# A hybrid mLSTM and convolution step on one core: other weight sums, places and pairings for the modulation and gate units of the first feed-forward

## The chip, the cores and the metric

The kernel runs on one core of a Trainium2 chip. Its engines are TensorE (PE; PEld is its weight load), VectorE (DVE), ScalarE (ACT), GpSimd (POOL) and SyncE (SP), which issues DMAs. Each works through its own queue in order; DMAs are issued from SP's and from POOL's queue. The metric is the device time of one execution in microseconds, the median of the runs.

## The reference, cut to what matters

One layer works on 128 context tokens and 512 latent tokens, 640 in all, of width 1024. The context is modulated with `c_ctx`, the latent tokens with `c`.

```python
mod = silu(cond) @ w_mod + b_mod                # 1024 x 9216, in nine chunks of 1024
sh1, sc1, g1, shm, scm, gm, sh2, sc2, g2 = split(mod, 9)
h = modulate(rmsnorm(x, norm_g[0]), sh1, sc1)
x = x + 0.5 * g1 * swiglu(h, ffn1_w1, ffn1_w2)  # D_FF = 2816
h = modulate(rmsnorm(x, norm_g[1]), shm, scm)
y = mixer(h, ...)                               # mLSTM and short convolution, merged, @ w_o
x = x + gm * y
h = modulate(rmsnorm(x, norm_g[2]), sh2, sc2)
x = x + 0.5 * g2 * swiglu(h, ffn2_w1, ffn2_w2)
y = rmsnorm(x, final_norm)

def modulate(h, shift, scale): return h * (1 + scale) + shift
def swiglu(h, w1, w2): a, b = split(h @ w1, 2); return (silu(a) * b) @ w2
```

So `shm` and `scm` are due when the first feed-forward ends, `g1` when its second matrix is multiplied, and `sh2` only after the mixer.

## The kernel before, in words

**Products.** Everything is kept with the features on the partitions and the 640 tokens along the free axis, in two halves of 320. Each float32 operand is split into a high and a low part (`split`, L75 the cast on ScalarE, L79 the difference on VectorE), and three matmuls of 320 columns (`three`, L288 to L290) make one float32 product.

**Pairs.** Most of the weights are multiplied two column blocks of 128 at a time (`pair_el`), by a two-by-two block scheme with seven products in place of eight (`pair_steps`): A11, S1, S2, A12, S3, S4, A22, each 4 x 3 = 12 matmuls, 84 a pair. S1 = A21 + A22, S2 = S1 + A11, S3 = A11 + A21 and S4 = A12 + S2 are sums of weight blocks, made by VectorE (L270; in the convolution's pairs S1 and S3 by GpSimd). The right side of each is a block of the activations, whose tile tells in the trace which product runs: H11, T1, T2, H21, T3, H22, T4. The products gather in four PSUM banks. S3 and A22 add into the same bank, and between the two the bank is read: by VectorE (L360), or, where the pair has `spare_v`, by ScalarE into a tile that VectorE then adds to. In the pairs of the second matrix the read is VectorE's L325, in `gated_sum`, unless `spare_v` is set.

**Summed pairs.** A pair marked `summed` gets S1 and S3 from the DMA: `pair_loads` loads two 256 KB quarters into a tile from SP's queue, adds two more to them with accumulating DMAs from POOL's queue (both L235), loads the first block (L218) as ever and the last quarter into a tile of its own, `wq`.

**Loads.** Weights come into a ring of five buffers of 512 KB (`wr`), in the order of the program; a load is issued when the buffer five places before it was given up (`load_more`). Splits are queued four products ahead of their use (`cast_more`, AHEAD = 4), so that in S3's step of a pair VectorE's queue gets the next pair's splits and sums ahead of L360.

**Modulation units.** A chunk of `mod` is computed half by half, in units of one 512 KB load of `w_mod` (L620). There are two ways. On VectorE (`mod_dve`): a unit has four steps, each a multiply-add over 512 columns into an accumulator (L765, L767); after a half's fourth unit TensorE adds up the partitions (L776), turns the result (L784), and VectorE adds the bias (L792). On TensorE (`mod_half`, wide, used by `with_own` for `g1`): a unit has two matmuls with 32 columns each (L649), in strips of 32 rows of one bank; even units use the first two strips, odd units the last two. In both ways the unit's load is put behind the loads of the pair that carries it and takes a place in the ring until its last step.

**Where steps go.** An element's `fill` is a list of steps; a pair issues them spread over its seven products, so that after product i some `len * i / 7` of them have been queued. `with_units` puts units into elements by the numbers in `places` and their closing steps (sum, turn, bias) into the elements after them.

**The first feed-forward** (`ffn`, called at the line that makes `head, els`) takes the 22 column blocks of the hidden layer in groups of 8, 8 and 6. In the first group three of the hidden blocks belong to the head, and five pairs follow; the first four carry the eight `g1` units. Each group of eight is multiplied with the second matrix in four pairs (`w2s`), whose results are added to `x` in DRAM by accumulating DMAs from POOL's queue (`x_add`, L1029). The last group has six pairs, 351.8 to 444.6 us in the trace, of which the third to the sixth are summed. In the first of them the last two `x_add` go out, and in the third `x` is loaded back (`x_in`, L2081, eight loads of 320 KB). Then five plain blocks of the second matrix and one element of three blocks in halves follow. Five halves made on VectorE, two of `shm`, two of `scm` and the first of `sh2`, are spread over all this as `places` says.

**The convolution** stands behind the mLSTM, 940 to 1113 us in the trace: ten pairs for its inputs (`bg_pair`, `cx_pair`) and four for a gate (`gsc_pair`).

Of the kernel before, what the change touches and what calls it, by code (L numbers as in the profile page):

```python
# [14 lines left out]
KT = 8  # L15
# [29 lines left out]
def mixer_step(ctx: ExitStack, tc: tile.TileContext, x_prompt, x_sample, state_C, state_n, state_m,  # L45
# [109 lines left out]
    def raw(n):  # L155
        load_more()
        return rtile[n]
# [40 lines left out]
    def step(fn):  # L198
        return element([], [], fn)
# [175 lines left out]
    def pair_el(load1, load2, ev, e1=None, spare_v=False, acts=HB, at=None, calm=False, gated=None,  # L375
                summed=False):
        po = pair_ops(summed, e1)
        at = at or {}

        def emit():  # L380
            nf = len(fill)
            for i, _ in enumerate(pair_steps(ORDER, ev, spare_v, acts, gated)):
                if not calm:
                    relax(7 - i if i else 9)
                drain(nf - nf * (i + 1) // 7)
                for f in at.get(i, ()):
                    f()
        return dict(element(pair_loads(load1, load2, summed), [po[name] for name in ORDER], emit), pair=True)
# [320 lines left out]
    def with_own(pairs, ch, *last):  # L709

        us, fs = zip(*[mod_half(ch, half, True) for half in range(2)])
        out = []
        for p, el in enumerate(pairs):
            el = dict(el, raws=list(el["raws"]))
            fill = []
            for i in (2 * p, 2 * p + 1) if p < 4 else ():
                load, unit_ = us[i // 4][i % 4]
                at_ = len(el["raws"])
                el["raws"].append(load)

                def go(unit_=unit_, at_=at_, el=el):
                    unit_(raw(el["base"] + at_))
                    rdone.add(el["base"] + at_)
                    load_more()
                fill += [step(go), step(lambda: None)]
            if p == 2:
                fill[1] = step(fs[0][0])
                fill[3:] = [step(f) for f in fs[0][1:]]
            if p == 4:
                fill = [step(fs[1][0]), step(lambda: None)] + [step(f) for f in (*fs[1][1:], *last)]  # L730
            el["fill"] = fill
            out.append(el)
        return out
# [68 lines left out]
    def with_units(main, units, spare=0, places=None):  # L802

        out = []
        n, m = len(main) - spare, len(units)
        e = 0
        post = []
        due = [sum(places[:i + 1]) for i in range(len(main))] if places else None
        for i, el in enumerate(main):
            el = dict(el, raws=list(el["raws"]), fill=list(el.get("fill", ())))  # L810
            now, post = post[:1], post[1:]
            if places:
                el["fill"], now = el["fill"] + now, []
            while e < m and (e < due[i] if places else e * n < (i + 1) * m):
                load, fns, more = units[e]
                at_ = len(el["raws"])
                el["raws"].append(load)
                for j, fn in enumerate(fns):
                    def go(fn=fn, at_=at_, el=el, last=(j == len(fns) - 1)):
                        fn(raw(el["base"] + at_))  # L820
                        if last:
                            rdone.add(el["base"] + at_)
                            load_more()
                    el["fill"].append(step(go))
                post += [step(f) for f in more]
                e += 1
            el["fill"] += now
            out.append(el)
        assert e == m
        return out + [step(lambda: lazy.extend(p["emit"] for p in post))]  # L830
# [212 lines left out]
    def eights(w1, w2, g, f0, n_head, head, more, back, sums, w2sums, pops_):  # L1043
# [76 lines left out]
        for m in range(0, KT, 2):  # L1120
            rows_ = lambda i, m=m: (tile_of((m + i) % 4), modT[:, g, m + i, 0:1])

            def ev(mi, h, src, m=m):
                y = tile_of((m + mi) % 4)
                if h and m == KT - 2:
                    PO["x_end"].append(lambda: x_add(m + mi, y))
                    return
                if h:
                    x_add(m + mi, y)
                    return  # L1130
                for a, b, cd in ((0, P, 1), (P, HT, 0)):
                    A.activation(y[:, a:b], src[:, a:b], AF.Copy, scale=modT[:, g, m + mi, cd:cd + 1])
            at = {}
            if m == 0:
                four = lambda k: lambda: put_lent("T4", k, raw2(k))
                at = {0: [lambda: relax_some(2)], 1: [relax], 2: [lambda: put_lent("T3", 3, raw3(3)), four(0)],
                      3: [four(1), four(2)], 4: [four(3)]}
            elif m == KT - 2 and back:
                at = {4: [lambda: h_back("T3")], 6: [lambda: h_back("T4")]}
            w2s.append(pair_el(w_load(w2, f0 * P, 8, m * P, D), w_load(w2, f0 * P, 8, (m + 1) * P, D), ev,  # L1140
                               acts=UB, at=at, gated=rows_, spare_v=m == 0, summed=m in w2sums))
        return grp, w2s

    def ffn(w1, w2, g, lists, head_of, n_head, groups, more, sums, w2sums, pops):
# [338 lines left out]
    def more_of(p):  # L1483
        return {0: {p: {0: [lambda: h_away("T3", "T4")]}}, 1: {0: {4: [x_end]}},
                2: {0: {4: [x_end, lambda: PO.pop("xs")]}, 2: {1: [x_whole]}}}
    head, els = ffn(ffn1_w1, ffn1_w2, G1, after_lists(1, SHM), first_head, 3, (8, 8, 6), more_of(4),
                    ({4, 5, 6, 7}, {4, 5, 6, 7}, {2, 3, 4, 5}), {0, 2}, {0: (2, 2, 1), 1: (2, 2, 1), 2: (3, 2)})
    PO["ma_x"] = ExitStack()

    def gate_weights_():  # L1490
# [5 lines left out]
    def ma_wide():  # L1496
# [3 lines left out]
    els[0][1][0] = dict(els[0][1][0], first=[open_ma, gate_weights_])  # L1500
    w2s = els[2][1]
    prog += with_units(els[0][1] + els[1][0] + els[1][1] + els[2][0] + w2s[:-1],
                       mod_dve(SHM, (0, 1), ma_wide) + mod_dve(SCM, (0, 1), ma_wide) + mod_dve(SH2, (0,), ma_wide),
                       places=[0, 2, 1, 0] + [1, 0, 0, 0, 1, 0, 0, 0] + [0, 2, 1, 1] + [1] * 6 + [1] * 5)
    prog += [step(gain(1, SCM)), step(lambda: PO["ma_x"].close()), w2s[-1]]


# [418 lines left out]
    def cx_pair(m):  # L1926
        def ev(mi, h, src):
            if mi == 0:
                CV["c", h] = t = t3()
                A.activation(t, src, AF.Identity, bias=bias(C_OFF + m * P))  # L1930
                return
            u = CV["c", h]
            V.scalar_tensor_tensor(u, src, bias(X_OFF + m * P), u, op0=OP.add, op1=OP.mult)
            if h == 0:
                CV[m] = xp.tile([P, T], F32, name="x", bufs=KT)
            uc = CV[m][:, hsl(h)]
            w0, w2 = col("cw", m), col("cw", 2 * KT + m)

            def mid():
                A.activation(uc, u, AF.Identity, scale=col("cw", KT + m), bias=col("cb", m))  # L1940

            def side(o, i, lo, hi, w):
                def f():
                    a, b = (o[:, :, 1:], i[:, :, :-1]) if lo else (o[:, :, :-1], i[:, :, 1:])
                    V.scalar_tensor_tensor(a, b, w, a, op0=OP.mult, op1=OP.add)
                return f
            segs = [(uc, u)] if h else [(uc[:, P:], u[:, P:])]
            segs = [(a.rearrange("p (r w) -> p r w", w=GW), b.rearrange("p (r w) -> p r w", w=GW))
                    for a, b in segs]
            if h == 0:  # L1950
                segs.append((uc[:, None, :P], u[:, None, :P]))
            lazy.insert(h, mid)
            for o, i in segs:
                lazy.extend([side(o, i, True, False, w0), side(o, i, False, True, w2)])
        return z_load(C_OFF + m * P), z_load(X_OFF + m * P), ev
# [77 lines left out]
    def bg_pair(m):  # L2033
        def ev(mi, h, src):
            uc = CV[m + mi][:, hsl(h)]
            V.scalar_tensor_tensor(uc, src, bias(B_OFF + (m + mi) * P), uc, op0=OP.add, op1=OP.mult)

            def put_b():
                PB[m + mi, h] = bpair()
                split(uc, *PB[m + mi, h])  # L2040
            lazy.append(put_b)
        return z_load(B_OFF + m * P), z_load(B_OFF + (m + 1) * P), ev
# [63 lines left out]
    ml[0]["fill"] = [step(f) for f in r_ins[6:]] + ml[0]["fill"] + [step(lambda: None)] * 5  # L2106
    prog.append(step(g_load(0)))
    prog += with_units(ml, mod_dve(GM, (1,), m_wide) + mod_dve(SH2, (1,), m_wide))
    for m in range(0, KT, 2):
        if m:  # L2110
            prog += [pair_el(*cx_pair(m), G), pair_el(*cx_pair(m + 1), G)]
        prog.append(pair_el(*bg_pair(m), G, spare_v=True))
    prog += weave([pair_el(*gsc_pair(m)) for m in range(0, KT, 2)], [step(lambda: None)] * 3 + [step(t_in(0))])
    y_acts = lambda k, h: YB[k, h]
    sc = [plain_el(w_load(w_sc_out, 0, KT, m * P, D), KT, lambda k, h: PB[k, h], sc_ev(m)) for m in range(KT)]
    for m in range(KT - 1):
# [126 lines left out]
```

## Time and profile before

| | |
|---|---|
| runs | 1665.88, 1674.21, 1669.24 us; median 1669.24 |
| profiled execution | 1670.03 us, its span 1667.9 us |
| mean granted TensorE clock | 0.993 |
| PE, DVE, ACT, POOL busy | 1628.7, 1301.8, 881.7, 337.7 us |
| bytes moved | 251.83 MB, 151 GB/s in the mean |

An instruction's row has its start, its length, engine, line, operation, and the tiles as out<-in; numbers of buffers are left out, so that `ps` is any product bank, `ax` any small one, `wr` any buffer of the ring, `ws` a sum of weights, `wh` and `wl` the halves of a split. A bracket behind it is the idle time of the engine before it and what ended that. Groups of waits name the waiting line, the line waited for, the total in us, the number of waits and the longest. The end of a matmul is modelled, and successive matmuls overlap, so starts are compared with starts.

### The profile page before, as it was taken

What the parts mean: (1) busy time and instruction counts of PE and PEld (TensorE: products, weight loads), DVE (VectorE), ACT (ScalarE), POOL (GpSimd) and SP (SyncE); (2) the same over time, 40 slices, a digit from 0 to 9 for tenths busy, and PEclk for the clock granted to TensorE, in tenths of its full rate; (3) what the DMA queues carried; (4) which work ended last, traced back from release to release, by engine and by line L of the source; (5) the groups of instructions that cost most, each with busy time, mean ns of one, the idle gap of its engine ahead of it and who ended that gap; (6) DMA issues with size and microseconds to landing.
All of it is one profiled execution on the core that took longest, in us unless ns stands there. A gap on an engine that the chain in (4) does not pass through costs nothing.

```text
span 1667.9 us, 29682 instructions
## 1 busy us (share of the span) xinstructions
PE 1628.7 (98%) x10997; PEld 1577.0 (95%) x10997; DVE 1301.8 (78%) x2730; ACT 881.7 (53%) x1953; POOL 337.7 (20%) x465
## 2 busy tenths in 40 slices
PE   8999999997989999999999999999999999999998
PEld 5989999997988999999999999999999999999998
DVE  6868878876768778787887788869778876786765
ACT  5656555643437665454653355642366665565443
POOL 2132311132011241111212222001123113113102
PEclk9999999998999999999999999999999999999999
DMA  9698966798535352343338532347558768468621
GB/s 322 182 239 171 222 151 130 174 215 215 154 94 177 95 134 69 92 107 83 105 92 298 148 89 77 104 137 227 153 161 182 144 147 199 96 150 184 180 80 63
DMA packets 339600, 251.83 MB, mean 151 GB/s; under 512 B 12019, under 2 KB 312442, under 8 KB 339456
## 3 DMA queue, kind: packets, MB, share of 16 engines
q1 hardware_dynamic: 280432, 169.89, 35.6%
q0 software_dynamic: 58992, 80.05, 22.5%
q8 instruction: 86, 1.41, 0.3%
q14 instruction: 58, 0.48, 0.1%
q10 hardware_dynamic: 32, 0.01, 0.0%
HBM read 213.62 MB, written 36.28 MB: 150 GB/s over the span
## 4 chain that ended last, share of the span: by engine, by line
PE 82%; DVE 8%; DMA 4%; ACT 4%; issue 2%; POOL 0%; SPq 0%; ACTq 0%; DVEq 0%; POOLq 0%
PE ps L288 25%; PE ps L289 24%; PE ps L290 24%; DMA wr<-in_ffn_w_dram 4%; DVE wl L79 2%; PE ax L1789 2%; PE ax L1820 2%; DVE ma L767 1%; PE ax L1792 1%; ACT wh L75 1%; DVE ws L270 1%; PE ax L1766 1%; ACT Uh L930 0%; DVE x L1016 0%; DVE HT4l L79 0%
## 5 line engine op out<-in xcount | busy, mean ns | idle before, releaser
L79 DVE TENSOR_TENSOR wl<-wr,wh 128x512 fp32r<-128x512 f32 (+1 forms) x401 | 277.7, 702 | 104.2 <-ACT wh L75 101.3
L75 ACT CAST wh<-wr 128x512 fp32r<-128x512 f32 (+1 forms) x403 | 238.3, 606 | 53.5 <-DMA wr<-in_ffn_w_dram 28.5
L79 DVE TENSOR_TENSOR wl<-ws,wh 128x512 fp32r<-128x512 f32 x300 | 207.0, 690 | 64.3 <-ACT wh L75 63.4
L75 ACT CAST wh<-ws 128x512 fp32r<-128x512 f32 x300 | 184.4, 621 | 94.2 <-DVE ws L270 82.1
L288 PE MATMUL ps<-HT4h,wh 128*128 128x320 f32 x440 | 140.7, 320 | 15.9 <-DVE t L360 13.2
L235 POOL DMA_DIRECT2D wr<-in_ffn_w_dram x56 | 72.7, 1469 | 329.8 <-DMA wr<-in_ffn_w_dram 167.2
L289 PE MATMUL ps<-HT4l,wh 128*128 128x320 f32 x440 | 137.7, 313 | 0.6 <-DVE HT4l L79 0.5
L288 PE MATMUL ps<-Uh,wh 128*128 128x320 f32 x440 | 138.2, 314 | 0.0
L290 PE MATMUL ps<-HT4h,wl 128*128 128x320 f32 x440 | 137.2, 312 | 0.0
L289 PE MATMUL ps<-Ul,wh 128*128 128x320 f32 x440 | 136.7, 311 | 0.0
L290 PE MATMUL ps<-Uh,wl 128*128 128x320 f32 x440 | 136.3, 310 | 0.0
L288 PE MATMUL ps<-HT3h,wh 128*128 128x320 f32 x388 | 121.8, 314 | 0.2
L288 PE MATMUL ps<-H11h,wh 128*128 128x320 f32 x376 | 119.1, 317 | 0.8 <-ACT H11h L75 0.8
L289 PE MATMUL ps<-HT3l,wh 128*128 128x320 f32 x388 | 119.9, 309 | 0.0
L290 PE MATMUL ps<-HT3h,wl 128*128 128x320 f32 x388 | 119.9, 309 | 0.0
L289 PE MATMUL ps<-H11l,wh 128*128 128x320 f32 x376 | 116.8, 311 | 0.7 <-DVE H11l L79 0.4
L288 PE MATMUL ps<-H21h,wh 128*128 128x320 f32 x376 | 117.5, 312 | 0.0
L290 PE MATMUL ps<-H11h,wl 128*128 128x320 f32 x376 | 116.3, 309 | 0.0
L290 PE MATMUL ps<-H21h,wl 128*128 128x320 f32 x376 | 116.2, 309 | 0.0
L289 PE MATMUL ps<-H21l,wh 128*128 128x320 f32 x376 | 115.9, 308 | 0.0
L288 PE MATMUL ps<-H22h,wh 128*128 128x320 f32 x344 | 107.7, 313 | 0.0
L289 PE MATMUL ps<-H22l,wh 128*128 128x320 f32 x344 | 106.4, 309 | 0.4
(489 smaller groups left out, 4954.2 us busy)
## 6 DMA issues: line engine op xcount, KB each, us to landing
wr<-in_ffn_w_dram SPq DMA_DIRECT2D x90, 512.0 KB, 5.8
wr<-in_w_in_dram SPq DMA_DIRECT2D x72, 512.0 KB, 3.9
wr<-in_w_mod_dram SPq DMA_DIRECT2D x59, 512.0 KB, 5.0
xd<-x POOLq DMA_DIRECT2D x56, 320.0 KB, 7.2
wr<-in_ffn_w_dram SPq DMA_DIRECT2D x60, 256.0 KB, 4.6
wr<-in_ffn_w_dram POOLq DMA_DIRECT2D x56, 256.0 KB, 5.3
x<-xd POOLq DMA_DIRECT2D x24, 320.0 KB, 7.7
wq<-in_ffn_w_dram SPq DMA_DIRECT2D x28, 256.0 KB, 3.2
```

The source lines that it names most:

```text
L75: A.copy(hi, raw)
L79: V.tensor_sub(lo, raw, f32(hi))
L235: queue.dma_start(t[:, 512 * o:512 * o + 512].rearrange("p (k n) -> p k n", k=4), dap(w, (row0 + 512 * half) * ncol + col0, [[ncol, P], [P ...
L270: engine.tensor_add(t, part(o, a), part(o, b))
L288: PE.matmul(ps, hi[:, ws], ah, start=start, stop=False, skip_group_check=True)
L289: PE.matmul(ps, hi[:, ws], al, start=False, stop=False, skip_group_check=True)
L290: PE.matmul(ps, lo[:, ws], ah, start=False, stop=stop, skip_group_check=True)
L767: V.scalar_tensor_tensor(acc, w_, s, acc, op0=OP.mult, op1=OP.add)
L1766: PE.matmul(p[:, :P], S["k", dt][:, sl], S["q", dt][:, sl], start=(dt == 0), stop=(dt == 1))
L1789: PE.matmul(p2[:, :DH + 1], S["q", dt][:, sl], S["C"][d][:, dt, :], start=(dt == 0), stop=(dt == 1))
L1792: PE.matmul(p1[:, :DH + 1], S["p", ch][:, d, :], PO["vt"][:, ch, :], start=True, stop=True)
L1820: PE.matmul(p[:, :DH + 1], kw[:, dt * P:(dt + 1) * P], PO["vt"][:, ch, :], start=True, stop=True)
```

## The change

It touches two places of the program. In the first feed-forward:

- Gate units in twos (`with_own`): the two `g1` units of a pair are issued in one step, behind the fifth product (in the third pair the fourth), not behind the second and the sixth. The steps that close the first half are moved with them.
- Modulation units early (`with_units`): where `places` is given, three empty steps follow each unit's four, so that a single unit's steps are queued behind the first four products of a pair, not behind the second, fourth, sixth and seventh.
- No DMA sums in the last group: its pairs load two blocks each, and VectorE makes all four sums.
- `spare_v` is set in two more of the four pairs of the second matrix in the groups of eight (`m` = 2 and 4).
- The four units of `sh2`'s first half leave the first feed-forward, and `places` is thinned: none in the last pair of the second group's second matrix, none in the last group's sixth pair, and the five plain blocks have one in the first three only.

In the convolution, these four units are put into the four `bg_pair` elements, with accumulators from the pool of `x` tiles; their closing steps go into the gate's pairs.

```diff
@@ with_own @@
             fill = []
-            for i in (2 * p, 2 * p + 1) if p < 4 else ():
-                load, unit_ = us[i // 4][i % 4]
+            if p < 4:
+                units = us[p // 2][2 * (p % 2):2 * (p % 2) + 2]
                 at_ = len(el["raws"])
-                el["raws"].append(load)
-
-                def go(unit_=unit_, at_=at_, el=el):
-                    unit_(raw(el["base"] + at_))
-                    rdone.add(el["base"] + at_)
+                el["raws"] += [load for load, _ in units]
+
+                def go(units=units, at_=at_, el=el):
+                    tiles = [raw(el["base"] + at_ + i) for i in range(2)]
+                    for i in range(2):
+                        units[i][1](tiles[i])
+                    rdone.update((el["base"] + at_, el["base"] + at_ + 1))
                     load_more()
-                fill += [step(go), step(lambda: None)]
+                fill = [step(lambda: None), step(go), step(lambda: None)]
             if p == 2:
-                fill[1] = step(fs[0][0])
-                fill[3:] = [step(f) for f in fs[0][1:]]
+                fill[0] = step(fs[0][0])
+                fill[2:] = [step(f) for f in fs[0][1:]]
@@ with_units @@
                 post += [step(f) for f in more]
+                if places:
+                    el["fill"] += [step(lambda: None)] * 3
                 e += 1
@@ eights @@
-                               acts=UB, at=at, gated=rows_, spare_v=m == 0, summed=m in w2sums))
+                               acts=UB, at=at, gated=rows_, spare_v=m == 0 or m < KT - 2 and 2 in w2sums, summed=m in w2sums))
@@ first feed-forward @@
-                    ({4, 5, 6, 7}, {4, 5, 6, 7}, {2, 3, 4, 5}), {0, 2}, {0: (2, 2, 1), 1: (2, 2, 1), 2: (3, 2)})
+                    ({4, 5, 6, 7}, {4, 5, 6, 7}, ()), {0, 2}, {0: (2, 2, 1), 1: (2, 2, 1), 2: (3, 2)})
@@
-                       mod_dve(SHM, (0, 1), ma_wide) + mod_dve(SCM, (0, 1), ma_wide) + mod_dve(SH2, (0,), ma_wide),
-                       places=[0, 2, 1, 0] + [1, 0, 0, 0, 1, 0, 0, 0] + [0, 2, 1, 1] + [1] * 6 + [1] * 5)
+                       mod_dve(SHM, (0, 1), ma_wide) + mod_dve(SCM, (0, 1), ma_wide),
+                       places=[0, 2, 1, 0] + [1, 0, 0, 0, 1, 0, 0, 0] + [0, 2, 1, 0] + [1, 1, 1, 1, 1, 0] + [1, 1, 1, 0, 0])
@@ convolution @@
+    conv = []
     for m in range(0, KT, 2):
         if m:
-            prog += [pair_el(*cx_pair(m), G), pair_el(*cx_pair(m + 1), G)]
-        prog.append(pair_el(*bg_pair(m), G, spare_v=True))
-    prog += weave([pair_el(*gsc_pair(m)) for m in range(0, KT, 2)], [step(lambda: None)] * 3 + [step(t_in(0))])
+            conv += [pair_el(*cx_pair(m), G), pair_el(*cx_pair(m + 1), G)]
+        conv.append(pair_el(*bg_pair(m), G, spare_v=True))
+    conv += weave([pair_el(*gsc_pair(m)) for m in range(0, KT, 2)], [step(lambda: None)] * 3 + [step(t_in(0))])
+    prog += with_units(conv, mod_dve(SH2, (0,), m_wide), places=[1, 0, 0] * 3 + [1] + [0] * 4)
```

## The prediction

> **What bounds the kernel now.** First the page: is one engine full, and where is it not?
>
> ```profile
> span 1667.9 us, 29682 instructions
> PE 1628.7 (98%) x10997; PEld 1577.0 (95%) x10997; DVE 1301.8 (78%) x2730; ACT 881.7 (53%) x1953; POOL 337.7 (20%) x465
> PEclk9999999998999999999999999999999999999999
> ```
>
> PE works for all but some 39 us, so work taken off the other engines pays only where PE waits for them. The granted clock dips in one slice, the tenth (375 to 417 us), inside the first feed-forward's last group. Next the waits, of PE alone, to see who makes it wait:
>
> ```profile
> PE ps L288 <- DVE t L360: 13.2, 4, 6.1
> PE ax L776 <- DVE ma L767: 4.5, 3, 3.2
> PE ps L288 <- DVE x L325: 2.1, 4, 0.8
> ```
>
> Three VectorE lines hold PE for 19.8 us, and the change touches all three. Then the table by stretches, with bounds put where PE's timeline shows matmuls of one pair or one gap. Columns: length, then busy time (and count) of PE, PEld, DVE, ACT, POOL; granted clock, DMA share, GB/s.
>
> ```profile
> 351.80:444.55 92.75, 79.52 (x519) 77.86 (x517) 61.91 (x114) 39.39 (x85) 20.80 (x26) 0.94 0.78 194
> 376.25:384.85 8.60, 3.84 (x15) 3.84 (x16) 5.30 (x10) 4.28 (x9) 3.26 (x6) 0.80 0.74 186
> 395.12:405.51 10.39, 4.29 (x18) 4.29 (x18) 6.42 (x12) 4.30 (x9) 2.64 (x2) 0.67 0.77 178
> 404.60:418.00 13.40, 13.40 (x94) 12.80 (x93) 9.46 (x18) 5.71 (x13) 0.00 (x0) 0.97 0.68 164
> 418.00:432.20 14.20, 12.78 (x88) 12.51 (x87) 10.19 (x19) 5.79 (x13) 2.57 (x2) 1.00 0.72 158
> 473.16:483.84 10.68, 5.82 (x24) 4.46 (x25) 7.02 (x15) 2.31 (x6) 2.53 (x4) 0.68 0.51 143
> 965.70:978.00 12.30, 12.30 (x86) 12.30 (x85) 10.82 (x20) 7.81 (x17) 2.87 (x2) 1.00 0.32 87
> 978.00:990.30 12.30, 12.30 (x86) 12.30 (x85) 11.95 (x21) 6.87 (x15) 2.83 (x2) 1.00 0.30 85
> 990.30:1002.60 12.30, 12.30 (x86) 12.30 (x85) 10.08 (x18) 6.58 (x14) 3.15 (x2) 1.00 0.33 87
> ```
>
> An undisturbed pair (965.70) is 12.30 us for 84 matmuls (two more overlap its edges): 0.146 us a matmul, 1.76 us a product of twelve. The last group's six pairs should take 6 x 12.30 = 73.8 us; they take 92.75. The two worst stretches follow in PE's, VectorE's and SyncE's timelines and in the chain:
>
> ```profile
> 381.01 0.42 PE L288 MATMUL ps<-HT4h,wh 128*128 128x320 f32 x1 [4.76 <-DVE t L360]
> 401.22 0.64 PE L288 MATMUL ps<-HT4h,wh 128*128 128x320 f32 x1 [6.10 <-DVE t L360]
> ...
> 378.66 0.69 DVE L79 TENSOR_TENSOR wl<-wr,wh 128x512 fp32r<-128x512 f32 x1 [6.85 <-ACT wh L75]
> 380.48 0.48 DVE L360 TENSOR_TENSOR t<-ps,t 128x320 f32<-128x320 f32 x1
> 385.58 0.74 DVE L767 SCALAR_TENSOR_TENSOR ma<-wr,cm,ma 128x512 f32<-128x512 f32 x1
> 398.21 0.69 DVE L79 TENSOR_TENSOR wl<-wr,wh 128x512 fp32r<-128x512 f32 x1 [8.01 <-ACT wh L75]
> ...
> 386.35 0.37 SPq L218 DMA_DIRECT2D wr<-in_ffn_w_dram  x1
> ...
> 386.35 11.18 DMA wr<-in_ffn_w_dram
> ```
>
> Read backwards: PE needs the bank that L360 reads; L360 stands in VectorE's queue behind the next pair's split, which waits for ScalarE's cast, which waits for a load. That load is issued at 386.35, the moment the modulation unit's last step (385.58 to 386.32) gives its buffer up, and takes 11.18 us to land. So the bound here is the ring of five buffers: a step queued behind a pair's seventh product keeps a load out.
>
> **The change part by part.** The profiled execution took 1670.0 us (span 1667.9 and 2.1 around it), 0.8 over the median, inside the runs' spread of 1665.9 to 1674.2. The sum is made against 1670.0.
>
> *Gate units in twos.* Four times, two of eight units go side by side after one product.
>
> ```profile
> 79.61 1.05 PE L649 MATMUL ax<-wr,cm 128*32 128x512 f32 x4
> 80.59 0.42 PE L288 MATMUL ps<-HT2h,wh 128*128 128x320 f32 x1
> ...
> 31.46 1.07 PE L649 MATMUL ax<-wr,cm 128*32 128x512 f32 x8
> 32.45 0.41 PE L288 MATMUL ps<-H11h,wh 128*128 128x320 f32 x1
> ...
> DMA to landing us min/median/max: 3.4/5.9/11.2
> ...
> PE ps L288 <- ACT t L357: 0.6, 1, 0.6
> ```
>
> One unit alone holds PE 0.98 us (79.61 to 80.59); the prologue's two together hold it 0.99 (31.46 to 32.45), since they write different 32-row strips of the bank. So 4 x 0.98 = 3.9 us go, all on PE's own path. A new wait comes in: both loads must have landed by the fifth product (in one pair the fourth), and the rest of the pair's matmuls stand behind the units in PE's queue. The second load is now issued behind the previous pair's fifth product instead of its second, still 12.3 us ahead; the third row, of the weight loads (L218) between 330 and 450 us, where the DMA engines are fullest, has 11.2 us at worst. On SyncE's queue this load now goes out just ahead of the next summed pair's two 256 KB loads, whose slot comes free one product earlier than before; I take 0 for that, between 0.6 won (the last row, PE's only other wait in this stretch) and 0.6 lost. Gain 3.9.
>
> *Last group: sums off, units early.* Removed: per summed pair two accumulating loads on POOL's queue and 512 KB. Added: two VectorE adds (L270) in four pairs. A pair's slots are now load, load, unit; the second load of the pair after next takes the unit's slot, and the unit's last step stands behind the fourth product, three products or 5.3 us earlier. From there to where that load is needed (the fifth product one pair on) lie 12.3 + 1.8 = 14.1 us. Before, 386.35 to the end of the product ahead of the gap (395.1) was 8.8.
>
> ```profile
> 383.11 4.88 POOL L2081 DMA_DIRECT2D x<-xd  x7
> L270 DVE TENSOR_TENSOR ws<-wr x130: 672/683/1168, 62.5 to 1598.1; 128x512 f32<-128x512 f32 x130
> L767 DVE SCALAR_TENSOR_TENSOR ma<-wr,cm,ma x70: 732/746/753, 165.6 to 477.0; 128x512 f32<-128x512 f32 x70
> ```
>
> Even a landing of 11.2 us fits into 14.1, though the burst of eight 320 KB loads on POOL's queue at 383, no longer held up there by the sums, stays and may take the margin of one. VectorE: the pair at 404.60 has 9.46 us of work with its unit; two adds of 0.68 make 10.8 of 12.3. It fits, but in-order waits will leave something: I take 0.3 us a pair for five pairs, 1.5 (bounds 0, and 6 if a pair is paced at 13.5). What goes: the 13.2 us of L360, and the slow clock behind it, 8.60 - 4.76 - 15 x 0.146 = 1.65 and 10.39 - 6.10 - 16 x 0.146 = 1.95 (two of the 18 belong to the product before). Net 13.2 + 3.6 - 1.5 = 15.3.
>
> Here the row and the Trainium skill weigh differently on what a remaining stall costs. By the rows the clock fell behind stalls of 4.76, 6.10 and 3.24 us and not behind 1.42 (418.00, clock 1.00); a stall between 1.42 and 3.24 may cost 0 to 1.9 us more. The Trainium skill, "TensorE: Matmul & The Clock Gate", Part 1, gives an idle window of about 3.4 us, free-running; by it such stalls would cost nothing more. The trace agrees in kind, but its 3.24 is a little under that window.
>
> *Four units from the group's end to the convolution.* PE's timeline behind 473.16:
>
> ```profile
> 476.40 0.63 PE L776 MATMUL ax<-ma,ones 128*32 128x256 f32 x4 [3.24 <-DVE ma L767]
> 477.85 1.07 PE L776 MATMUL ax<-ma,ones 128*32 128x256 f32 x4 [0.82 <-DVE ma L767]
> 479.71 0.69 PE L784 MATMUL ax<-ident,t 128*128 128x128 f32 x2 [0.80 <-ACT t L779]
> ```
>
> The reduction of the last accumulators stands between the last two blocks with nothing left to cover VectorE's lateness. Of the stretch's 24 matmuls, 8 + 2 are these and 14 x 0.146 = 2.05 us feed-forward work; 10.68 - 2.05 = 8.6 us go, slow clock included. The same ten matmuls come back in the convolution, where PE is full: about 1.0 us at full clock (0.63 for the strips side by side, half of 0.69 for the transposes). The rest of L776's 4.5 (0.4) goes too, for the reduction that stays now follows a block later than its last unit. Net 8.6 + 0.4 - 1.0 = 8.0. The two last blocks before 473 lose four steps of 0.75 us each, so VectorE has caught up by then, and nothing else stands behind that wait.
>
> In the convolution four pairs get 4 x 0.75 = 3.0 us of VectorE steps. The pair at 978.00 has 11.95 busy already: 14.95 in 12.30, 2.65 late. The pair behind it (10.08) wins back 2.2 over its length, 1.6 by its fifth product.
>
> ```profile
> 980.07 1.53 POOL L270 TENSOR_TENSOR ws<-wr 128x512 f32<-128x512 f32 x1 [8.04 <-DVE ws L270]
> 980.82 1.13 DVE L1933 SCALAR_TENSOR_TENSOR t<-t,biT,t 128x320 f32<-128x320 f32 x1
> 999.31 0.49 DVE L360 TENSOR_TENSOR t<-ps,t 128x320 f32<-128x320 f32 x1
> ```
>
> L360 of that pair starts at 999.31 with no delay today; 1.05 late plus its own 0.49 just about uses up the one product (1.76) before PE needs the bank. I take 0.6 us for each of two such pairs, 1.2; bounds 0 and 8.0 (three pairs paying 2.65). PSUM is safe otherwise: these pairs copy it out on ScalarE.
>
> *Two more pairs of each 8-wide group's second matrix read PSUM by ScalarE.* L325's 2.1 us of waits were VectorE's queue; with the copy on ScalarE (53% busy) PE waits for that alone, but ScalarE's casts, ahead of it in its queue, wait for VectorE's adds. I take 1.7 of 2.1 (bounds 0 and 2.1). The units in these pairs issue the same steps, only earlier: 0.
>
> Sum: 3.9 + 15.3 + 8.0 + 1.7 - 1.2 = 27.7; 1670.0 - 27.7 = 1642.3.
>
> **The rivals.**
> *One late load remains* (15%): the burst at 383 still catches one pair; a stall like that at 376.25 (8.60 - 2.20 = 6.4) stays: 1648.7. For: landings to 11.2 us. Against: 14.1 us of room.
> *VectorE becomes the bound* (15%): the last group pays 6 instead of 1.5 and the convolution 8.0 instead of 1.2: 1653.6. For: 11.95 of 12.30 busy, and the step at 980.82, as wide as L360 (0.49), which takes 1.13 beside a GpSimd add that runs to 981.60. Against: 10.8 of 12.3 in the group.
> *It doesn't do what it says* (7%): not the slot but full DMA engines (share 0.78) make the loads late, and the group's stalls only move: the 15.3 is lost, 1657.6.
> *Slower* (3%): without the sums each pair waits for 1 MB and a unit on one queue, and loads land later than 14 us in every pair. All six then pay as at 395.12, 10.39 - 2.34 = 8.05: 48.3 instead of 1.5, so 1689. Against: a pair with its unit needs 3 x 512 KB = 1.57 MB in 12.3 us, 128 GB/s, and the group as it is moves 194.
>
> **How the numbers follow.** The forecast has 60%; its own bounds (0 instead of 1.5 and 1.2, 2.1 instead of 1.7) reach to 1639 and, with the runs' spread, 1636. The range goes up over the first two rivals to 1655 and leaves out the last two. About 0.5% is what a measurement of this kernel can tell from no change: 1660.9 and below is faster. The first three cases lie there, and of the fourth half: 0.60 + 0.15 + 0.15 + 0.04 = 0.94. Slower is the last rival, 0.03; the rest 0.03.
>
> **What would show it.** Right: L649 as x8 in about 1 us, four times, between 75 and 125 us; no wait of PE on L360 over 1.5 us and a clock of 1.00 in the last group, its six pairs in about 76 us; no L776 between the last two blocks; the moved reduction's L776 in the convolution's last pairs. Wrong: an L360 wait over 3 us there, or in the convolution; a PE wait on a load at L649; VectorE idle on a DMA ahead of L270 in every pair.

## The result, and the profile after

The changed kernel takes 1645.56 us, the median of four runs (1645.25 to 1645.99); the kernel before took 1670.80 in the four runs beside it (1665.88 to 1674.21). The ratio is 0.9851, with a 95% interval of 0.9825 to 0.9878. The forecast was 1642.3. The profiled execution took 1645.83 us, with a span of 1643.9, 24.0 below the span before. Two executions further down, one of the kernel before with 3935 us and one of the last kernel with 4082, lie far outside all others; the ratios leave them out, and they move the medians by at most 0.6.

The page of the changed kernel, then its waits of PE alone:

```profile
span 1643.9 us, 29669 instructions
PE 1620.0 (99%) x10997; PEld 1573.2 (96%) x10997; DVE 1308.9 (80%) x2738; ACT 883.1 (54%) x1957; POOL 325.5 (20%) x457
```

```profile
PE ps L288 <- DVE t L360: 4.0, 3, 3.1
```

L360's 13.2 us have become 4.0, of which 3.1 is one stall. No row is left of the reduction (L776 before, L778 now) or of L325. Now the table by stretches (length; busy time and count of PE, PEld, DVE, ACT, POOL; clock, DMA share, GB/s), first of before, then of after. A stretch begins at the same product in both kernels. In order: the second matrix of the first group, of the second group, the last group's six pairs, the blocks at its end, the convolution with the products just ahead of it.

```profile
148.75:199.97 51.22, 50.13 (x338) 49.28 (x337) 43.45 (x77) 30.55 (x69) 13.47 (x21) 1.00 0.85 197
299.55:351.79 52.24, 51.12 (x346) 49.43 (x345) 44.48 (x78) 31.00 (x70) 11.55 (x16) 1.00 0.83 194
351.79:444.55 92.76, 79.53 (x519) 77.87 (x517) 61.92 (x114) 39.39 (x85) 20.80 (x26) 0.94 0.78 194
444.55:500.96 56.41, 50.50 (x338) 46.74 (x336) 41.42 (x90) 19.29 (x44) 8.13 (x9) 0.94 0.39 110
881.93:1094.05 212.12, 211.72 (x1450) 210.08 (x1449) 173.36 (x300) 103.77 (x208) 41.73 (x44) 1.00 0.46 134
```

```profile
144.64:194.54 49.90, 49.88 (x339) 49.29 (x337) 43.13 (x77) 31.30 (x71) 13.65 (x21) 1.00 0.86 204
294.00:344.57 50.57, 50.49 (x347) 49.33 (x345) 44.14 (x77) 31.47 (x71) 12.03 (x18) 1.00 0.86 205
344.57:425.80 81.23, 78.12 (x521) 77.05 (x517) 63.47 (x115) 40.22 (x86) 9.59 (x17) 0.96 0.59 174
425.80:472.40 46.60, 46.00 (x329) 44.35 (x326) 36.26 (x80) 19.05 (x43) 8.21 (x9) 1.00 0.34 100
853.37:1069.97 216.60, 214.56 (x1461) 210.70 (x1459) 185.43 (x316) 103.48 (x209) 42.05 (x44) 1.00 0.48 141
```

The first column of numbers gives the account. That all before the second matrix is 4.1 shorter is read from where the first rows begin (148.75 and 144.64).

| stretch | after less before, us | forecast |
|---|---|---|
| up to the first group's second matrix (gate units) | -4.1 | -3.9 |
| second matrix, both groups | -1.3 - 1.7 = -3.0 | -1.7 |
| last group | -11.5 | -15.3 |
| its end | -9.8 | -9.0 |
| convolution | +4.5 | +1.0 + 1.2 = +2.2 |
| all else | -0.1 | 0 |
| sum | -24.0 | -27.7 |

Three terms are mis-sized: the last group and the convolution to the worse, the second matrix to the better. The last group's one stall, by PE's timeline, the chain of waits, POOL's and VectorE's timelines, and the table around it:

```profile
371.02 0.64 PE L288 MATMUL ps<-HT4h,wh 128*128 128x320 f32 x1 [3.11 <-DVE t L360]
```

```profile
353.89 0.49 DVE t L360
354.38 0.67 DVE ma L769
...
355.07 12.31 DMA wr<-in_ffn_w_dram
...
367.40 0.07 DVE ws L270
```

```profile
351.75 3.30 POOL L2085 DMA_DIRECT2D x<-xd  x6 [0.17 <-issue]
355.74 0.54 POOL L2085 DMA_DIRECT2D x<-xd  x1 [0.68 <-DMA xd<-x]
358.98 0.54 POOL L2085 DMA_DIRECT2D x<-xd  x1 [2.71 <-DMA xd<-x]
```

```profile
367.40 0.69 DVE L270 TENSOR_TENSOR ws<-wr 128x512 f32<-128x512 f32 x1 [4.15 <-DMA wr<-in_ffn_w_dram]
...
370.48 0.48 DVE L360 TENSOR_TENSOR t<-ps,t 128x320 f32<-128x320 f32 x1
```

```profile
367.91:375.90 7.99, 4.88 (x19) 4.88 (x19) 7.11 (x14) 3.55 (x7) 0.00 (x0) 0.63 0.30 85
```

The load goes out at 355.07, right behind the unit's last step. That step stands behind L360 in VectorE's queue, about 3 us later than the forecast had it: the fourth product is over at 351.93, where PE starts the fifth. And the eight 320 KB loads of x, which had gone out at 383 before, now go out from 351.75 on, and the weight load lands only after 12.31 us. From its landing VectorE needs 3.6 us (367.40 to the end of L360 at 370.96) until PE is free. Then the clock is low: 19 matmuls take 4.88 us instead of 19 x 0.146 = 2.77, 2.1 more. Stall and clock cost 5.2.

### The profile page after: what moved, and what is told of

The parts are those of the page before. It is cut to its first block, busy times and chain, and to the rows that moved or that the text cites. A ratio compares the mean times of both kernels' runs of the same rounds, so it can differ in the third digit from the quotient of the medians.

```text
span 1643.9 us, 29669 instructions
## 1 busy us (share of the span) xinstructions
PE 1620.0 (99%) x10997; PEld 1573.2 (96%) x10997; DVE 1308.9 (80%) x2738; ACT 883.1 (54%) x1957; POOL 325.5 (20%) x457
## 4 chain that ended last, share of the span: by engine, by line
PE 84%; DVE 6%; DMA 3%; ACT 3%; issue 2%; SPq 1%; POOL 0%; ACTq 0%; DVEq 0%; POOLq 0%
PE ps L288 26%; PE ps L289 25%; PE ps L290 25%; DMA wr<-in_ffn_w_dram 3%; DVE wl L79 2%; PE ax L1793 2%; PE ax L1824 2%; PE ax L1796 1%; ACT wh L75 1%; PE ax L1770 1%; DVE ws L270 1%; ACT Uh L934 0%; SPq L627 0%; DVE Uh L926 0%; PE ax L778 0%
## 5 line engine op out<-in xcount | busy, mean ns | idle before, releaser
L79 DVE TENSOR_TENSOR wl<-ws,wh 128x512 fp32r<-128x512 f32 x308 | 212.9, 691 | 62.9 <-ACT wh L75 62.5
L75 ACT CAST wh<-ws 128x512 fp32r<-128x512 f32 x308 | 189.1, 620 | 97.9 <-DVE ws L270 83.2
L235 POOL DMA_DIRECT2D wr<-in_ffn_w_dram x48 | 62.3, 1448 | 282.6 <-DMA wr<-in_ffn_w_dram 115.9
```

The lines of the kernel that those rows point to most:

```text
L75: A.copy(hi, raw)
L79: V.tensor_sub(lo, raw, f32(hi))
L235: queue.dma_start(t[:, 512 * o:512 * o + 512].rearrange("p (k n) -> p k n", k=4), dap(w, (row0 + 512 * half) * ncol + col0, [[ncol, P], [P ...
```

## The experiments

Four kernels at a time ran on one chip beside the kernel before. The medians of before were 1670.74, 1672.51 and 1666.68 in the three sets, so times are compared within a set; the first set holds the kernel before alone as its control, and there the ratios are compared.

**Set 1, which edit frees the last group.** *The sums off alone*: the kernel before with

```diff
-                    ({4, 5, 6, 7}, {4, 5, 6, 7}, {2, 3, 4, 5}), {0, 2}, ...
+                    ({4, 5, 6, 7}, {4, 5, 6, 7}, ()), {0, 2}, ...
```

> The kernel before with one part of the change: no DMA sums in the last group. Units stay late, places stay. Slot theory (the unit's late last step keeps a load out of the ring): the second load of a pair still waits for the end of the pair two before, so with the x loads now going out early at least one stall of 3 to 5 us stays and the group takes 80 to 84 us instead of 92.8; total 1657 to 1661. Traffic theory (the bytes and the accumulating DMAs of the sums made the loads late): no L360 wait over 1.5 us, group 75 to 77 us, total 1652 to 1655. Neither: over 1666.

*The units early alone*: the kernel before with

```diff
+                if places:
+                    el["fill"] += [step(lambda: None)] * 3
                 e += 1
```

> The kernel before with one part of the change: three empty steps behind each unit's four, so that units are queued early; the sums stay in the DMA. Slot theory: the load behind the unit's slot goes out about 5 us earlier, the stalls of 4.8 and 6.1 us go or shrink to one of at most 3, the group takes 76 to 82 us, total 1655 to 1662. Traffic theory: the same bytes, so both stalls stay within 1 us of what they were, total 1667 or more.

Measured: 1661.29 (1660.25 to 1662.77), ratio 0.9941 [0.9914, 0.9968], and 1655.98 (1655.36 to 1657.84), ratio 0.9904 [0.9876, 0.9932]. PE's waits on L360, of the sums off, then of the units early:

```profile
PE ps L288 <- DVE t L360: 4.0, 1, 4.0
```

```profile
PE ps L288 <- DVE t L360: 6.0, 1, 6.0
```

POOL's timelines, where the x loads begin, in the same order:

```profile
359.70 1.91 POOL L2081 DMA_DIRECT2D x<-xd  x2
```

```profile
376.33 2.59 POOL L235 DMA_DIRECT2D wr<-in_ffn_w_dram  x2 [7.99 <-DMA wr<-in_ffn_w_dram]
377.85 4.89 POOL L2083 DMA_DIRECT2D x<-xd  x7
```

The second experiment speaks for the slot: with every byte of the DMA sums still moved, the earlier unit alone wins 14.8 us, where the traffic theory gave at least 1667. Traffic is not without part, though: either edit alone leaves one long stall of L360 in place of four waits, and the second one's, of 6.0 us where at most 3 was expected, stands at the end of a pair that had none before (399.7 to 405.7), behind a load of 9.05 us. They are two ways to much the same gain: 9.4 and 14.8 here, and 25 for the whole change, other parts included. And without the sums the x loads go out at 359.70; with them they stand in POOL's queue behind an accumulating load that waits for its base load, until 377.85. So it is the removal of the sums that brings the x loads forward.

*The x loads held back*: the changed kernel, with a GpSimd copy ahead of the x loads that reads a late tile of the last group's fourth pair.

```diff
-                        sa[h] = t3()
+                        sa[h] = PO["sa"] = t3()
...
+    def x_late():
+        G.tensor_copy(tp.tile([P, 3], F32, name="rstd", bufs=2)[:, 0:1], PO["sa"][:, 0:1])
+        x_whole()
...
-                2: {0: {...}, 2: {1: [x_whole]}}}
+                2: {0: {...}, **({3: {6: [x_late]}} if p == 4 else {2: {1: [x_whole]}})}}
```

> The changed kernel, with the eight loads of x held back on the POOL queue until a tile of the last group's fourth pair is written (a copy of one column on GpSimd stands ahead of them). Burst theory (the one stall left, 3.1 us of PE waiting on L360 and half clock behind it, comes from a weight load issued while the eight x loads run): the stall goes, no L360 wait over 1 us in the last group, group about 75 to 76 us, total 1639 to 1641. Rival (that load is late for its slot alone): the stall stays above 2 us, total 1644 to 1647. If x then comes too late for the plain blocks: a wait on x there, total over 1646.

Measured: 1645.23 (1641.19 to 1646.29), ratio 0.9833 [0.9797, 0.9870]. By the time the rival would have it; the trace says otherwise. The whole last group by the table, then POOL's timeline, then PE's waits:

```profile
348.85:424.47 75.62, 75.55 (x521) 74.47 (x517) 63.16 (x115) 40.34 (x86) 10.71 (x19) 1.00 0.65 187
```

```profile
398.84 4.33 POOL L2089 DMA_DIRECT2D x<-xd  x8
```

```profile
PE ps L288 <- ACT t L357: 3.5, 1, 3.5
```

With x going out at 398.84 PE works 75.55 of 75.62 us at full clock: the stall is gone, and the group is 5.6 us shorter than in the changed kernel (81.23). The missing time is another wait, of 3.5 us on L357 in the first pairs (at 115.4), where this kernel is the same program as the changed one.

*Both units of a gate pair on the same strips*: the changed kernel with

```diff
-                units = us[p // 2][2 * (p % 2):2 * (p % 2) + 2]
+                units = us[p // 2][p % 2::2]
```

> The changed kernel, with the two gate units of a pair chosen so that both write the same two 32-row strips (first and third, then second and fourth). Strips theory (two units together cost as much as one because they use different strips): the eight matmuls take about 1.9 us instead of 1.07, four times, total 1649 to 1650. Rival (the gain comes from fewer switches between the two kinds of matmul): about 1.1 us as in the changed kernel, total 1645 to 1646.5.

Measured: 1647.81 (1646.51 to 1649.23), ratio 0.9854 [0.9825, 0.9882]. The chain, of the changed kernel and of this one, around the first two units:

```profile
85.06 1.00 PE ax L649 x8
```

```profile
85.27 1.84 PE ax L649 x8
```

Two units take 1.00 us on different strips and 1.84 on the same ones, so the saving is the strips' work side by side, not fewer switches. Four times 0.84 are 3.4. The time alone would not have shown it: it lies between the two theories, and its ratio is that of the changed kernel (0.9851), since the wait in the first pairs varies by more; in this execution it was absent.

**Set 2, with the changed kernel as control.**

> The changed kernel once more, as the control for the next three. With the x loads held, the stall at 367.9 was gone (5.7 us won from the first matmul of that product on), but 4.2 us were lost in the first pairs at 115.7, where a weight load landed 3.2 us later than in the changed kernel, though nothing differs there. If that loss comes and goes with the run or the chip, the changed kernel pays it here in some runs too: 1645 to 1650, wider than its first four runs (1645.25 to 1645.99). If it belongs to holding the loads, the control stays at 1645 to 1646.5.

Measured: 1648.86 (1646.76 to 1653.12), ratio 0.9867 [0.9842, 0.9892]; the profiled execution took 1653.12. So the wait belongs to the changed kernel itself and comes and goes. PE's timeline, the chain, and the table around it, in that execution:

```profile
120.71 0.63 PE L288 MATMUL ps<-HT4h,wh 128*128 128x320 f32 x1 [4.84 <-ACT t L357]
```

```profile
100.47 10.15 DMA wr<-in_ffn_w_dram
...
111.28 8.41 DMA wr<-in_ffn_w_dram
...
119.71 0.62 ACT wh L75
120.33 0.33 ACT t L357
```

```profile
115.87:127.00 11.13, 6.29 (x27) 6.29 (x27) 5.99 (x13) 2.96 (x6) 2.59 (x2) 0.69 0.88 165
```

The chain of the kernel before at the same place:

```profile
104.02 6.99 DMA wr<-in_ffn_w_dram
...
111.39 7.04 DMA wr<-in_ffn_w_dram
...
118.44 0.62 ACT wh L75
```

Read both: a summed pair's base load, the accumulating load on top of it, the cast on ScalarE, and in ScalarE's queue behind that cast the copy L357 that frees PE's bank. The chain ended at 118.4 before and at 119.7 here. The gate units in twos bring PE there 3 us sooner (the stall begins at 115.87 instead of 118.9), so it waits for what was just in time, and may lose the clock as well (0.69).

*The convolution's units in other pairs*: the changed kernel with

```diff
-    ... places=[1, 0, 0] * 3 + [1] + [0] * 4)
+    ... places=[1, 1, 0, 0, 1, 0, 0, 1, 0, 0] + [0] * 4)
```

> Of the four moved units in the convolution the first stays in the first pair; the others go from the fourth, seventh and tenth pair to the second, fifth and eighth. Theory: the three waits of about 1 us each in the convolution come because the pairs that were given a unit had 11.95 us of VectorE work in 12.3 already; in the other pairs (10.1 us) the unit fits, so 2 to 3 us are won: 1642.5 to 1644. Rival: VectorE is short over the whole stretch and the lateness is only passed on: 1645 to 1646.5.

Measured: 1646.94 (1646.19 to 1649.17), ratio 0.9857 [0.9828, 0.9886]. The trace shows no gain in the convolution: the waits move to 975.9 and 1014.3, 1.20 us each, and over the whole stretch the kernel is 0.2 slower than the changed one. That fits the rival: lateness is passed on. The 1.9 below the control are put down to the first pairs' and the last group's waits, which vary; that is not shown.

*Both mends together* (x held, these places):

> x loads held back as in the third experiment and the convolution's units as in the sixth, together. If each gain stands alone (5.7 and 2 to 3): 1637 to 1638.5 where the first pairs do not stall, 1641 to 1643 where they do. If holding x always costs those 4 us in the first pairs: 1641 to 1643 in every run.

Measured: 1645.22 (1643.98 to 1646.70), ratio 0.9845 [0.9816, 0.9874]: 3.6 below the control, but above both expectations (1643 at most). In the profiled execution the last group takes 75.6 us by its matmuls' starts and the convolution gains nothing; the first pairs paid 2.7 us on L357.

*The moved units put back* into the last group:

```diff
-                       mod_dve(SHM, (0, 1), ma_wide) + mod_dve(SCM, (0, 1), ma_wide),
-                       places=[0, 2, 1, 0] + [1, 0, 0, 0, 1, 0, 0, 0] + [0, 2, 1, 0] + [1, 1, 1, 1, 1, 0] + [1, 1, 1, 0, 0])
+                       mod_dve(SHM, (0, 1), ma_wide) + mod_dve(SCM, (0, 1), ma_wide) + mod_dve(SH2, (0,), ma_wide),
+                       places=[0, 2, 1, 0] + [1, 0, 0, 0, 1, 0, 0, 0] + [0, 2, 1, 1] + [1] * 6 + [1] * 5)
-    prog += with_units(conv, mod_dve(SH2, (0,), m_wide), places=...)
+    prog += conv
```

> The changed kernel with the four units back in the feed-forward group (places as before) and none in the convolution; all else as changed. By the differences of the two traces the move brings 9.8 us at the group's end and costs 4.4 in the convolution, net 5.4: 1650.5 to 1652. By the forecast's terms it brings 9.0 and costs 2.2 in all, net 6.8 of which the early units have part: 1652 to 1654. If the early and free last group already takes the end's wait away, the move is worth nothing or less: 1641 to 1646.

Measured: 1653.32 (1652.23 to 1660.52), ratio 0.9899 [0.9873, 0.9926], 4.5 above the control. In its trace the last reduction stands between the last blocks again:

```profile
458.10 0.63 PE L778 MATMUL ax<-ma,ones 128*32 128x256 f32 x4 [2.39 <-DVE ma L769]
```

So the move is worth 4.5 net: less than the 6.8 of the forecast, near the 5.3 of the two traces (9.8 - 4.5, the control's own waits being in the difference). By the matmuls' starts of this kernel the group's end takes 55.7 us and the convolution 212.6, so the move itself brings 9.1 at the end (55.7 - 46.6) and costs 4.0 (216.6 - 212.6).

**Set 3.** The control once more:

> The changed kernel as the control for the next three: 1645 to 1650. In its second control a stall of 4.84 us stood at 115.9 in the first pairs, with the clock at half behind it; the chain before it runs over the base load of a summed pair (10.15 us), the accumulating load on top of it (8.41), a cast on ScalarE and the copy that frees a PSUM bank.

Measured: 1646.41 (1645.38 to 1651.52), ratio 0.9881 [0.9858, 0.9905]; in the profiled execution, its fastest, L357 held PE for 0.9 us.

*The gate units singly again*, with all else as changed (`with_own` as before the change):

> The changed kernel with the gate units singly again, as before the change. By the forecast they cost 3.9 us: 3.5 to 4.5 above the control. Theory now: the loads of the summed pair at 115 end at about 119 whether the units come singly or in twos (118.4 before, 119.7 in the control), so the 3 us that two pairs have saved by then are waited for instead, and the half clock behind the stall costs more: only 0 to 2.5 above the control, and no stall over 1 us between 110 and 130.

Measured: 1649.11 (1648.17 to 1650.74), ratio 0.9891 [0.9868, 0.9914]: 2.7 above the control, between the two theories. Its profile shows no wait on L357 at all, and behind the first pairs its matmuls start some 4 us later than those of the changed kernel's profile. The control's runs spread over 6.1 us, these over 2.6. So twos win about 4 us of PE's time, and the accumulating chain takes a part back, another one each time. With a spread of 6.1 in the control, the 2.7 is a difference of medians and not a sure size.

*One summed pair less* in the first group:

```diff
-                    ({4, 5, 6, 7}, {4, 5, 6, 7}, ()), {0, 2}, ...
+                    ({4, 5, 7}, {4, 5, 6, 7}, ()), {0, 2}, ...
```

> The changed kernel with plain loads instead of accumulating ones for that one pair (the fourth on the list of the first group), 0.75 MB less, two VectorE adds more. If the accumulating chain makes the stall at 115.9: no stall over 1 us between 110 and 130 in the profile, and 2 to 6 below the control. If full DMA engines make it (share 1.24 there, the hidden halves being written out), the stall is only smaller: within 2 of the control.

Measured: 1647.02 (1644.37 to 1647.95), ratio 0.9874 [0.9853, 0.9896]. No stall over 1 us stands there:

```profile
110.50:127.00 16.50, 16.23 (x111) 14.90 (x111) 14.01 (x29) 9.37 (x21) 2.66 (x2) 1.00 0.89 219
```

But the median is not below the control's (1646.41), and the control's profile had only 0.9 there too. By the time it is the case of the rival, within 2 of the control. The runs lie closer together (3.6 against 6.1 us, none above 1648), which fits the theory and doesn't prove it. That the accumulating chain makes the wait is read from the chain; that one plain pair mends it is not shown.

*Three mends* (x held, one summed pair less, the convolution's last unit two pairs later):

> x loads held (third experiment), one summed pair less (as above), and the last of the convolution's units two pairs later. If the gains add up (5.7 in the last group, 3 to 5 in the first pairs, about 1 in the convolution): 1636 to 1639, the shortest of all. If the DMA engines are the common cause and a stall only moves: above 1641.

Measured: 1642.95 (1639.63 to 1642.99), ratio 0.9848 [0.9822, 0.9874]. It beats the kernel before, and the changed one by 3.5 on the same chip, but misses the 1636 to 1639 expected and lies where the rival put it, above 1641. In its profile the last group and the first pairs run without a stall of PE, and the convolution is 1.0 shorter by its matmuls' starts. But a wait stands there that the changed kernel's profile does not have: 1.20 us on ScalarE's step L2021, behind a load of 6.94 us on POOL's queue at 844.36, with a low clock after it, 2.9 us in all by the matmuls' starts. So a stall did come up elsewhere, as the rival has it; why that load is late here was not tried.

## Why the prediction was right, and where its terms failed

*The total.* 27.7 us forecast, 24.0 between the two profiled executions. That it came so near is in part luck: two controls of the changed kernel had medians of 1648.86 and 1646.41, 20 to 24 us below the kernel before on their chips, and the errors of the terms partly cancel. The signs named for the last group failed: an L360 wait over 3 us was named as a sign of being wrong, and one of 3.11 stands there, with a clock of 0.96 and 81.2 us for the six pairs. The other signs of being right came.

*What bounds.* Right in the main: with the traffic unchanged, the earlier slot alone wins 14.8 us. But with the slot unchanged, the sums off win 9.4, and a load beside the x burst is slow in both kernels (11.18 us at 386.35 before, 12.31 at 355.07 now). So the slot bounds, and the traffic says how long a landing takes. The rival that the change doesn't do what it says (1657.6) falls by the measured time and the second experiment.

*Gate units in twos*: 3.9 forecast, 4.1 in the profiled execution. The step that failed is the zero taken for the new order of loads, "between 0.6 won ... and 0.6 lost". The row quoted for it, 0.6 us of L357, was itself the sign that the accumulating chain ended just when PE came; reaching it 3 us earlier cost between nothing and 4.8 us of waiting in the runs, and 2.7 is what the edit was worth by medians. That the profiled execution shows 4.1 is luck: in it the chain ended early, and L357 held PE for only 0.2.

*Last group*: 15.3 forecast, 11.5 measured. The step that failed is "even a landing of 11.2 us fits into 14.1". The rival *one late load remains* was right about the burst, and saw it at 383: the sums that the change removes were what held the x loads there, so the change moved them to 351.75, onto the weight load (12.31 us). And the room was not 14.1. It began at 355.07, 3.1 us late, since the unit's last step stood behind L360; and it ended 3.6 us before PE's stall begins at 367.91, since VectorE needs that long from the landing to the end of L360. From 355.07 to 364.35 are 9.3 us: even the 11.2 would not have fitted. Stall and clock cost 3.1 + 2.1 = 5.2; with x held they came back (5.6). The 1.5 taken for VectorE's residue was not there: undisturbed, in the third experiment, the group takes 75.62, 17.1 below the 92.76 of before, and PE idles 0.07 us of it.

*What a stall costs.* "A stall between 1.42 and 3.24 may cost 0 to 1.9 us more": 3.11 cost 2.1. The Trainium skill, "TensorE: Matmul & The Clock Gate", Part 1, ties the fall to a free-running idle window of about 3.4 us. A free-running window of that length fits the traces (last section); that a whole window has to be idle does not, since 2.67 us were enough, and there the measurement decides.

*The group's end*: 8.6 + 0.4 = 9.0 forecast, 9.8 measured. With the move undone the end is still 0.7 shorter than before, so the move is worth 9.1 there, and the rest of the change 0.7. The reduction's own matmuls in the convolution take 0.64 + 0.38 = 1.0, as forecast.

*Convolution*: 1.2 forecast, 4.5 - 1.0 = 3.5 measured. The unit's size, "4 x 0.75 = 3.0 us of VectorE steps", was right for the stretch: VectorE's busy time rose by 12.1 us for four units (173.36 to 185.43). A single step can be longer. VectorE's and POOL's timelines of the changed kernel there:

```profile
953.33 0.74 DVE L769 SCALAR_TENSOR_TENSOR x<-wr,cm,x 128x512 f32<-128x512 f32 x1
...
954.92 1.78 DVE L769 SCALAR_TENSOR_TENSOR x<-wr,cm,x 128x512 f32<-128x512 f32 x1
```

```profile
954.80 1.35 POOL L270 TENSOR_TENSOR ws<-wr 128x512 f32<-128x512 f32 x1 [1.75 <-issue]
```

A step that meets GpSimd's add takes 1.78. The prediction had quoted such a step (1.13 where L360 takes 0.49). The Trainium skill, "SBUF — State Buffer", section "SBUF: two separate sides", describes it: VectorE with two SBUF inputs and GpSimd take turns at a shared port pair, an instruction at a time; the trace agrees (0.74 + most of 1.35). But in the kernel before GpSimd's adds met other steps of VectorE (as at 980.82), so its total grew by no more than the plain steps.

The term that was mis-sized is what this lateness costs PE: "0.6 us for each of two such pairs", at L360 alone, with "PSUM is safe otherwise". The chain and PE's waits of the changed kernel:

```profile
959.99 0.66 DVE x L769
...
963.32 0.41 DVE t L367
```

```profile
PE ps L288 <- ACT ps L332: 0.6, 1, 0.6
```

By the matmuls' starts each of the two pairs (961.81 and 999.94) lost 1.2. Of that, 0.7 goes at L360's product and 0.5 at the pair's first products; the chain at the first of them comes from L367, VectorE's last read of a bank for the pair before, which stands in its queue behind the unit. The pair behind the fourth unit, the gate's first, which the forecast does not count, lost 0.9 more: PE waits there 0.64 for ScalarE's copy L332, which stands behind a cast that waits for VectorE's sum. The sixth experiment shows that another place for the units does not help.

*Second matrix*: 1.7 forecast (at most 2.1), 3.0 measured. The second experiment, which has the early units and not the ScalarE copies, is 0.6 faster in these stretches by its matmuls' starts; the other 2.4 lie 0.3 above the bound, which counted only waits that the list names.

## What to carry to other kernels

When a change removes work from a queue, ask what that work was holding back: the transfers behind it start earlier, and land on whatever moves there. A wait of half a microsecond at the end of a chain of loads is a chain that is just in time, so a gain ahead of it is paid out only up to that chain's end. Count the room of a load up to the first engine that needs it, not up to TensorE.

## What the hardware showed that was not expected

The clock can fall after a shorter stall and stay up after a longer one. PE's timeline and the table, first with one summed pair less (eleventh experiment), then with the gate units singly (tenth):

```profile
371.94 0.48 PE L288 MATMUL ps<-HT4h,wh 128*128 128x320 f32 x1 [2.67 <-DVE t L360]
```

```profile
368.74:372.15 3.41, 0.74 (x5) 0.48 (x4) 3.41 (x7) 1.24 (x2) 0.00 (x0) 1.00 0.38 98
372.15:375.56 3.41, 3.41 (x14) 3.41 (x14) 2.52 (x6) 1.70 (x4) 0.00 (x0) 0.50 0.51 142
```

```profile
375.19 0.41 PE L288 MATMUL ps<-HT4h,wh 128*128 128x320 f32 x1 [2.94 <-DVE t L360]
```

```profile
370.49:373.90 3.41, 1.76 (x13) 1.49 (x11) 2.33 (x4) 0.62 (x1) 0.00 (x0) 1.00 0.91 264
373.90:377.31 3.41, 2.12 (x14) 2.12 (x15) 2.90 (x6) 1.09 (x3) 0.00 (x0) 1.00 0.05 16
```

A stall of 2.67 us lost clock (0.50 for the next 3.41 us), one of 2.94 did not (1.00). So below 3 us the same wait may cost its own length or some 1.5 us more.

The record of the clock shows what the two have apart. Within each run the changes of the clock lie whole multiples of 3.41 us from each other, and the stretches above are steps of that grid, counted from other changes of the same run. The stall of 2.67 lies in one step, which is idle for 2.67 of its 3.41 us; the edge at 373.90 splits the one of 2.94 into 1.65 and 1.29. In the fourteen traces, between 60 and 1630 us, every step at full clock in which PE's rows leave at least 1.97 us idle was followed by half clock, and none with 1.82 or less but one (1.60 idle, in the last kernel). This is read from the traces; no run was made to test it.
